# Splitting float32 weights into two interleaved halves, with activation tiles at shifted addresses, in a two-layer encoder

## The chip, the cores and the metric

The kernel runs on one core of one Trainium2 chip. The metric is the device time of one execution in microseconds (us); less is better.

## The reference, cut to what matters

A trunk of two layers on 512 tokens of width 1024, all in float32. Each layer is a pre-norm mixer with a residual add, and a last RMS norm closes the trunk. Layer 0 projects to a value and a gate half of width 2048 each, pools the values over trailing windows, mixes them by group, multiplies by the gate and projects back. Layer 1 (HGRN2) projects to four parts of width 2048 (query, forget gate, value, gate), runs a gated linear recurrence over 16 heads, and projects back.

```python
def pool_mixer(h, w_in, w_grp, scale, w_out):
    v, gate = split(h @ w_in)
    p = multiscale_pool(v)
    m = einsum('btgc,gcd->btgd', p, w_grp).reshape(B, T, D_INNER) * scale
    return (m * silu(gate)) @ w_out

def hgrn2_mixer(h, w_in, lb, norm_g, w_out):
    q, fz, i, gate = split(h @ w_in)
    o = scan(q, k(fz), i, log_f(fz))      # S_t = f_t S_(t-1) + k_t v_t, o_t = S_t q_t
    return (norm(o) * silu(gate)) @ w_out
```

## The kernel before

All products with weights are done as three matmuls. A float32 operand is split in a high half (the value rounded to the type float32r, which TensorE takes in one pass) and a low half (what is left): `split` (L93) lets ScalarE (ACT) cast the source to `hi` and VectorE (DVE) subtract `hi` from the source into `lo`. `mm3` (L125) then adds high by high (L126), high by low (L127) and low by high (L128) into one PSUM tile:

```python
def mm3(out, lh, ll, rh, rl, start, stop):
    nc.tensor.matmul(out, lh, rh, start=start, stop=False)
    nc.tensor.matmul(out, lh, rl, start=False, stop=False)
    nc.tensor.matmul(out, ll, rh, start=False, stop=stop)
```

The first operand of a matmul is the stationary one: 128 columns of it are loaded into the array by a weight load of its own (PEld in the profile). The second is the moving one, 512 columns here. In the profile's names, `mm<-xh,whi` is the moving `xh` and the stationary `whi`.

Weights come in pieces of 128 partitions by 1024 float32 columns (`piece`, L97; the first four pieces are loaded half by half at L219 to L230). Each piece has a raw tile `wraw` (4,096 bytes of each partition, 3 buffers) and two halves `whi` and `wlo` (4,096 bytes each, 6 buffers each), all of the pool `wpool`. SP's queue issues the load at L103 as soon as a raw buffer is free, ahead of its place in the program (`high_priority`).

The activations of a layer are scaled by the norm's gain and split in eight pairs `xh0`, `xl0` .. `xh7`, `xl7` of 512 columns (2,048 bytes) by `scaled_halves` (L197), once for each layer, in the pool `act`. `project` (L144) makes an output tile of 128 features by 512 tokens by running over the eight (or four) contraction tiles k with the weights stationary and the activations moving. `project4` does it for four output tiles at once, with k outermost. Three places have the roles turned, with activations stationary and weights moving: `inputs` (L394, the values of layer 1) and `out_half` (L345), which `add_out` and `finish` call. Between the products, DVE, ACT and GpSimd (POOL) work on the rows that come out (pooling, sigmoids, the recurrence's factors); TensorE also does the small 128-column products of the recurrence and the transposes.

SBUF is laid out pool after pool, tile after tile: 1,024 bytes of scratch for DMA descriptors, then `const`, `wpool`, `act`, `small`, and then the pool of the layer (`l0`, or the one of layer 1 in its place). Adding up the tiles' sizes gives their place in each partition. Taken modulo 256 bytes, the start of `whi` and `wlo` is 128, that of all `xh` and `xl` is 128, that of the pooled tiles `ph`, `pl` and the gated tiles `zh`, `zl` of layer 0 is 0, that of `z1h`, `z1l` of layer 1 is 128, and the pair `zz` of the last group is at 192 (high) and 0 (low). Slices within a tile start at multiples of 512 bytes.

Of the kernel before, what the change touches and what calls it, by code (L numbers as in the profile page):

```python
# [32 lines left out]
F32 = mybir.dt.float32  # L33
F32R = mybir.dt.float32r
# [6 lines left out]
P = 128  # L41
# [3 lines left out]
KD = D // P  # L45
KI = DI // P
NG = 4
GC = DI // NG
# [2 lines left out]
EPS = 1e-6  # L51
WINDOWS = (2, 4, 8, 16)
RAW, WB = 3, 6
WARM = 10
NORM_AT, SPREAD_AT = (KD - 2, 2), (KD - 1, 1)
AHEAD = 300
# [9 lines left out]
def trunk(ctx: ExitStack, tc: tile.TileContext, xT, par, ident_d, causal_d, mask_d, fg_d, w0_in, w0_grp, w0_out, w1_in, w1_out, out):  # L66
    nc = tc.nc
    const = ctx.enter_context(tc.tile_pool(name="const", bufs=1))
    wpool = ctx.enter_context(tc.tile_pool(name="wpool", bufs=1))
    act = ctx.enter_context(tc.tile_pool(name="act", bufs=1))  # L70
# [9 lines left out]
    warm = pa.tile([P, 512], F32, name="a", tag="a", bufs=4)  # L80
    for _ in range(WARM):
        nc.tensor.matmul(warm[:, :P], ones, ones, start=True, stop=True)
# [3 lines left out]
    nc.scalar.dma_start(out=pp, in_=par)  # L86
    ident = const.tile([P, P], F32, name="ident")
    mhalf = const.tile([P, 8], F32, name="mhalf")
    nc.gpsimd.memset(mhalf, -0.5)

    h = [const.tile([P, T], F32, name=f"h{k}") for k in range(KD)]

    def split(src, hi, lo):  # L93
        nc.scalar.copy(out=hi, in_=src)  # L94
        nc.vector.tensor_tensor(out=lo, in0=src, in1=hi, op=ALU.subtract)  # L95

    def piece(src):  # L97

        raw = wpool.tile([P, 2, GC], F32, name="wraw", tag="wraw", bufs=RAW)
        hi = wpool.tile([P, 2, GC], F32R, name="whi", tag="whi", bufs=WB)  # L100
        lo = wpool.tile([P, 2, GC], F32R, name="wlo", tag="wlo", bufs=WB)
        with tc.high_priority(AHEAD):
            nc.sync.dma_start(out=raw, in_=src)  # L103
            split(raw, hi, lo)
        return hi, lo

    def load_in(w, col=0):

        v = w.rearrange("(k p) n -> p k n", p=P)
        out = []  # L110
        for i in range(v.shape[1] // 2):
            hi, lo = piece(v[:, 2 * i:2 * i + 2, col:col + GC])
            out += [(hi[:, 0], lo[:, 0]), (hi[:, 1], lo[:, 1])]
        return out
# [15 lines left out]
    def project4(pieces, xs, norm):  # L130


        accs = [ps.tile([P, T], F32, name="mm", tag="mm", bufs=4) for _ in range(GT)]
        for k, ((wh, wl), (xh, xl)) in enumerate(zip(pieces, xs)):
            for n, acc in enumerate(accs):
                if (k, n) == NORM_AT:
                    rn = norm()
                if (k, n) == SPREAD_AT:
                    rb = spread_sbuf(rn)
                c = slice(n * P, (n + 1) * P)  # L140
                mm3(acc, wh[:, c], wl[:, c], xh, xl, k == 0, k == len(pieces) - 1)
        return accs, rn, rb

    def project(pieces, n, xs):  # L144

        acc = ps.tile([P, T], F32, name="mm", tag="mm", bufs=4)
        c = slice(n * P, (n + 1) * P)
        for k, ((wh, wl), (xh, xl)) in enumerate(zip(pieces, xs)):
            mm3(acc, wh[:, c], wl[:, c], xh, xl, k == 0, k == len(pieces) - 1)
        return acc  # L150
# [40 lines left out]
    def spread_sbuf(rn):  # L191
# [2 lines left out]
        nc.scalar.copy(out=rb, in_=spread(rn))  # L194
        return rb

    def scaled_halves(k, col):  # L197
        g = pp[:, col + k:col + k + 1]
        hi = act.tile([P, T], F32R, name=f"xh{k}", tag=f"xh{k}", bufs=1)
        lo = act.tile([P, T], F32R, name=f"xl{k}", tag=f"xl{k}", bufs=1)  # L200
        nc.scalar.activation(out=hi, in_=h[k], func=AF.Copy, scale=g)
        nc.vector.scalar_tensor_tensor(out=lo, in0=h[k], scalar=g, in1=hi, op0=ALU.mult, op1=ALU.subtract)
        return hi, lo

    def halves(src, tag, bufs, pool=act):
        hi = pool.tile([P, T], F32R, name=tag + "h", tag=tag + "h", bufs=bufs)
        lo = pool.tile([P, T], F32R, name=tag + "l", tag=tag + "l", bufs=bufs)
        split(src, hi, lo)
        return hi, lo
# [7 lines left out]
    with tc.tile_pool(name="l0", bufs=1) as l0:  # L217
        xs, pieces = [], []
        wv = w0_in.rearrange("(k p) n -> p k n", p=P)  # L219
        for i in range(4):  # L220
            raw = wpool.tile([P, 2, GC], F32, name="wraw", tag="wraw", bufs=RAW)
            hi = wpool.tile([P, 2, GC], F32R, name="whi", tag="whi", bufs=WB)
            lo = wpool.tile([P, 2, GC], F32R, name="wlo", tag="wlo", bufs=WB)
            for j in range(2):
                k = 2 * i + j
                nc.sync.dma_start(out=h[k], in_=xT[k * P:(k + 1) * P, :])
                nc.sync.dma_start(out=raw[:, j], in_=wv[:, k, 0:GC])
                xs.append(scaled_halves(k, C_NG0))
                split(raw[:, j], hi[:, j], lo[:, j])
                pieces.append((hi[:, j], lo[:, j]))  # L230
        nc.scalar.dma_start(out=ident, in_=ident_d)
        accs, _, rb = project4(pieces, xs, lambda: rms("l0", h))
        cnts = [C_CNT + sum(WINDOWS[:g]) for g in range(NG)]

        def values(g):
            vs = []
            wv = None if g == 0 else load_in(w0_in, g * GC)
            for n in range(GT):
                acc = accs[n] if g == 0 else project(wv, n, xs)
                v = l0.tile([P, 16 + T], F32, name="v", tag="v", bufs=4)  # L240
                nc.gpsimd.memset(v[:, 0:16], 0.0)
                nc.vector.tensor_tensor(out=v[:, 16:], in0=acc, in1=rb, op=ALU.mult)
                vs.append(v)
            return vs

        def pool(g, vs):
            w, out = WINDOWS[g], []
            for n in range(GT):
                cur, step = vs[n], 1
                while step < w:  # L250
                    nxt = l0.tile([P, 16 + T], F32, name="win", tag="win", bufs=2)
                    if 2 * step < w:
                        nc.gpsimd.memset(nxt[:, 0:16], 0.0)
                    nc.vector.tensor_tensor(out=nxt[:, 16:], in0=cur[:, 16:], in1=cur[:, 16 - step:16 + T - step], op=ALU.add)
                    cur, step = nxt, 2 * step
                nc.vector.tensor_tensor(out=cur[:, 16:16 + w], in0=cur[:, 16:16 + w], in1=pp[:, cnts[g]:cnts[g] + w], op=ALU.mult)
                p = small.tile([P, T], F32, name="p", tag="hg", bufs=2)
                nc.vector.scalar_tensor_tensor(out=p, in0=cur[:, 16:], scalar=1.0 / w, in1=vs[n][:, 16:], op0=ALU.mult, op1=ALU.subtract)
                out.append(halves(p, "p", 4, l0))
            return out  # L260

        def gates0(g):
            wg = load_in(w0_in, DI + g * GC)
            out = []
            for n in range(GT):
                acc = project(wg, n, xs)
                gt = l0.tile([P, T], F32, name="gt", tag="gt", bufs=2)
                nc.vector.tensor_tensor(out=gt, in0=acc, in1=rb, op=ALU.mult)
                sg = l0.tile([P, T], F32, name="sg", tag="sg", bufs=2)
                nc.scalar.activation(out=sg, in_=gt, func=AF.Sigmoid)  # L270
                gs = l0.tile([P, T], F32, name="gs", tag="gs", bufs=4)
                nc.gpsimd.tensor_tensor(out=gs, in0=gt, in1=sg, op=ALU.mult)  # L272
                out.append(gs)
            return out

        def mixed(g, ps_, gates):
            wm = load_in(w0_grp[g])
            out = []
            for n in range(GT):
                acc = project(wm, n, ps_)  # L280
                z = small.tile([P, T], F32, name="z", tag="hg", bufs=2)
                c = C_PS + g * GT + n
                nc.vector.scalar_tensor_tensor(out=z, in0=acc, scalar=pp[:, c:c + 1], in1=gates[n], op0=ALU.mult, op1=ALU.mult)
                out.append(halves(z, "z", 8, l0))
            return out

        zprev = None
        for g in range(NG):
            vs = values(g)
            px = pool(g, vs)  # L290
            if zprev is not None and g < NG - 1:
                project_out(load_out(w0_out, g - 1), zprev)
            gts = gates0(g)
            z = mixed(g, px, gts)
            if g == NG - 1:
                project_out(load_out(w0_out, g - 1), zprev)
            zprev = z
        project_out(load_out(w0_out, NG - 1), zprev)
# [482 lines left out]
```

## Time and profile before

| | us |
|---|---|
| median of 2 runs (842.31 to 843.68) | 842.99 |
| the profiled execution, its own time | 843.0 |
| its span in the profile | 841.2 |

Times in the rows below count from the start of the span. A matmul's duration in them overlaps the next one's; what tells how fast a row of matmuls runs is the distance between starts. The granted clock is a share of full speed: 1.00 is 2.4 GHz.

### The profile page before, as it was taken

To read this page: it belongs to the slowest core of one execution; us is meant where nothing else is said; L and a number is where in the kernel's file an instruction comes from. 1 tells how busy PE (TensorE), PEld (TensorE's weight loads), DVE (VectorE), ACT (ScalarE), POOL (GpSimd) and SP (SyncE) were. 2 spreads that over 40 slices of the span, in tenths; PEclk is the share of its full clock that TensorE was granted. 3 is DMA by queue.
4 is the path that set the end of the run, shared out by engine and by line. 5 is a ranking of instruction groups with operands and counts; after the bars stand their busy time and mean duration, and the time that the engine had idled before them with its cause. 6 is when DMAs were issued, how large, how long until landed. Compare 5 with 4: busy or idle time off the path is not lost.

```text
span 841.2 us, 10459 instructions
## 1 busy us (share of the span) xinstructions
PE 826.4 (98%) x4038; PEld 684.8 (81%) x4038; DVE 550.9 (65%) x837; ACT 275.2 (33%) x474; POOL 160.6 (19%) x204
## 2 busy tenths in 40 slices
PE   9899999999999999999999999999999999999995
PEld 7688888888888888888888888888888888888884
DVE  7766645753686456699269974459974459973744
ACT  7342224213323145323433240433240433242311
POOL 4020001001002013071223300213300213302100
PEclk9999999999999999999999999999999999999998
DMA  6622323122422245223032240332240333230202
GB/s 218 213 75 77 100 101 101 53 98 101 150 82 97 75 151 175 76 76 125 1 101 79 71 141 10 101 101 87 80 135 1 101 101 92 82 128 1 101 13 91
DMA packets 37194, 79.06 MB, mean 94 GB/s; under 512 B 2832, under 2 KB 3088, under 8 KB 37136
## 3 DMA queue, kind: packets, MB, share of 16 engines
q1 hardware_dynamic: 34688, 74.46, 27.1%
q10 hardware_dynamic: 2448, 3.86, 1.3%
q8 instruction: 33, 0.54, 0.3%
q14 instruction: 25, 0.20, 0.1%
HBM read 74.11 MB, written 4.19 MB: 93 GB/s over the span
## 4 chain that ended last, share of the span: by engine, by line
PE 95%; DVE 1%; DMA 1%; ACT 1%; issue 0%; POOL 0%; SPq 0%; POOLq 0%; DVEq 0%; ACTq 0%
PE mm L126 29%; PE mm L127 29%; PE mm L128 29%; PE a L556 2%; PE a L594 2%; PE a L574 1%; PE a L596 1%; PE a L563 1%; DMA wraw<-in_w0i 1%; PE a L438 1%; DVE wlo L95 1%; DMA h<-in_xT 0%; PE a L342 0%; ACT whi L94 0%; PE a L188 0%
## 5 line engine op out<-in xcount | busy, mean ns | idle before, releaser
L126 PE MATMUL mm<-xh,whi 128*128 128x512 f32 x640 | 251.2, 393 | 1.3 <-ACT whi L94 0.7
L128 PE MATMUL mm<-xh,wlo 128*128 128x512 f32 x640 | 249.7, 391 | 1.0 <-DVE wlo L95 1.0
L127 PE MATMUL mm<-xl,whi 128*128 128x512 f32 x640 | 249.7, 390 | 0.0
L94 ACT CAST whi<-wraw 128x1024 fp32r<-128x1024 f32 (+1 forms) x140 | 141.9, 1025 | 252.3 <-PE mm L127 115.5
L95 DVE TENSOR_TENSOR wlo<-wraw,whi 128x1024 fp32r<-128x1024 f32 (+1 forms) x140 | 172.7, 1261 | 57.6 <-ACT whi L94 56.6
L126 PEld LDWEIGHTS mm<-xh,whi 128*128 128x128 f32 x640 | 120.6, 188 | 27.1 <-ACT whi L94 1.4
L128 PEld LDWEIGHTS mm<-xh,wlo 128*128 128x128 f32 x640 | 120.4, 188 | 27.2 <-DVE wlo L95 2.0
L127 PEld LDWEIGHTS mm<-xl,whi 128*128 128x128 f32 x640 | 120.5, 188 | 24.5
L541 DVE RECIPROCAL r<-r 128x512 f32<-128x512 f32 x16 | 53.4, 3340 | 1.5 <-POOL r L540 1.5
L128 PE MATMUL mm<-zh,wlo 128*128 128x512 f32 x128 | 50.6, 395 | 0.0
L126 PE MATMUL mm<-zh,whi 128*128 128x512 f32 x128 | 50.6, 395 | 0.0
L127 PE MATMUL mm<-zl,whi 128*128 128x512 f32 x128 | 50.5, 395 | 0.0
L126 PE MATMUL mm<-whi,xh 128*128 128x512 f32 x128 | 50.1, 391 | 0.0
L128 PE MATMUL mm<-whi,xl 128*128 128x512 f32 x128 | 49.9, 390 | 0.0
L127 PE MATMUL mm<-wlo,xh 128*128 128x512 f32 x128 | 49.9, 390 | 0.0
L351 DVE TENSOR_TENSOR ht<-mm,ht 128x512 f32<-128x512 f32 x32 | 22.1, 689 | 35.5 <-PE mm L128 35.5
L214 DVE TENSOR_TENSOR h<-mm,h 128x512 f32<-128x512 f32 x32 | 22.0, 689 | 32.4 <-PE mm L128 32.3
L414 POOL TENSOR_TENSOR gs<-fz,s 128x512 f32<-128x512 f32 x16 | 21.4, 1336 | 98.6 <-ACT s L412 98.6
L272 POOL TENSOR_TENSOR gs<-gt,sg 128x512 f32<-128x512 f32 x16 | 21.3, 1330 | 92.4 <-ACT sg L270 92.3
L126 PE MATMUL mm<-whi,z1h 128*128 128x512 f32 x96 | 37.6, 392 | 0.0
L128 PE MATMUL mm<-whi,z1l 128*128 128x512 f32 x96 | 37.4, 389 | 0.0
L127 PE MATMUL mm<-wlo,z1h 128*128 128x512 f32 x96 | 37.4, 389 | 0.0
(141 smaller groups left out, 1164.9 us busy)
## 6 DMA issues: line engine op xcount, KB each, us to landing
wraw<-in_w1i SPq DMA_DIRECT2D x64, 512.0 KB, 3.9
wraw<-in_w0i SPq DMA_DIRECT2D x28, 512.0 KB, 4.2
wraw<-in_w0o SPq DMA_DIRECT2D x16, 512.0 KB, 3.9
wraw<-in_w1o SPq DMA_DIRECT2D x16, 512.0 KB, 4.3
wraw<-in_w0g SPq DMA_DIRECT2D x8, 512.0 KB, 4.1
h<-in_xT SPq DMA_DIRECT2D x8, 256.0 KB, 5.0
wraw<-in_w0i SPq DMA_DIRECT2D x8, 256.0 KB, 5.2
hmid<-h ACTq DMA_DIRECT2D x8, 256.0 KB, 2.3
```

The costliest lines, as they stand in the source:

```text
L94: nc.scalar.copy(out=hi, in_=src)
L95: nc.vector.tensor_tensor(out=lo, in0=src, in1=hi, op=ALU.subtract)
L126: nc.tensor.matmul(out, lh, rh, start=start, stop=False)
L127: nc.tensor.matmul(out, lh, rl, start=False, stop=False)
L128: nc.tensor.matmul(out, ll, rh, start=False, stop=stop)
L214: nc.vector.tensor_tensor(out=h[n], in0=acc, in1=h[n], op=ALU.add)
L272: nc.gpsimd.tensor_tensor(out=gs, in0=gt, in1=sg, op=ALU.mult)
L351: nc.vector.tensor_tensor(out=ht[b][:, c], in0=acc, in1=ht[b][:, c], op=ALU.add)
L414: nc.gpsimd.tensor_tensor(out=gs, in0=gt, in1=sg, op=ALU.mult)
L541: nc.vector.reciprocal(out=r, in_=r)
L556: nc.tensor.matmul(a[0:64, b], k[:, c:m], q[:, c:c + P], start=True, stop=True)
L594: nc.tensor.matmul(o[:, b], Ads[pr][:, j, t], v[:, b, n * P:(n + 1) * P], start=True, stop=b == 0)
```

## The change

The high and low half of a weight piece stand in one tile of 8,192 bytes, element by element: high half at every even float32, low half at every odd one. `hi` and `lo` are views of it with a step of 8 bytes, in all that reads or writes them. The order and number of instructions stay as they are. In `scaled_halves`, an unused tile of 32 bytes is allocated after each pair but the last, so that pair k starts 32·k bytes further than it would; both layers use the same tiles. A pad of 128 bytes in `const` and a DMA scratch that is 512 bytes smaller shift everything behind them.

```diff
--- before.py
+++ after.py
@@ -51,6 +51,7 @@
 EPS = 1e-6
 WINDOWS = (2, 4, 8, 16)
 RAW, WB = 3, 6
+PAD = 32
 WARM = 10
 NORM_AT, SPREAD_AT = (KD - 2, 2), (KD - 1, 1)
 AHEAD = 300
@@ -86,6 +87,7 @@
     nc.scalar.dma_start(out=pp, in_=par)
     ident = const.tile([P, P], F32, name="ident")
     mhalf = const.tile([P, 8], F32, name="mhalf")
+    const.tile([P, PAD], F32, name="pad")
     nc.gpsimd.memset(mhalf, -0.5)
 
     h = [const.tile([P, T], F32, name=f"h{k}") for k in range(KD)]
@@ -97,8 +99,8 @@
     def piece(src):
 
         raw = wpool.tile([P, 2, GC], F32, name="wraw", tag="wraw", bufs=RAW)
-        hi = wpool.tile([P, 2, GC], F32R, name="whi", tag="whi", bufs=WB)
-        lo = wpool.tile([P, 2, GC], F32R, name="wlo", tag="wlo", bufs=WB)
+        both = wpool.tile([P, 2, GC, 2], F32R, name="wb", tag="wb", bufs=WB)
+        hi, lo = both[..., 0], both[..., 1]
         with tc.high_priority(AHEAD):
             nc.sync.dma_start(out=raw, in_=src)
             split(raw, hi, lo)
@@ -194,10 +196,15 @@
         nc.scalar.copy(out=rb, in_=spread(rn))
         return rb
 
+    staggered = set()
+
     def scaled_halves(k, col):
         g = pp[:, col + k:col + k + 1]
         hi = act.tile([P, T], F32R, name=f"xh{k}", tag=f"xh{k}", bufs=1)
         lo = act.tile([P, T], F32R, name=f"xl{k}", tag=f"xl{k}", bufs=1)
+        if k < KD - 1 and k not in staggered:
+            staggered.add(k)
+            act.tile([P, 8], F32, name=f"step{k}")
         nc.scalar.activation(out=hi, in_=h[k], func=AF.Copy, scale=g)
         nc.vector.scalar_tensor_tensor(out=lo, in0=h[k], scalar=g, in1=hi, op0=ALU.mult, op1=ALU.subtract)
         return hi, lo
@@ -219,8 +226,8 @@
         wv = w0_in.rearrange("(k p) n -> p k n", p=P)
         for i in range(4):
             raw = wpool.tile([P, 2, GC], F32, name="wraw", tag="wraw", bufs=RAW)
-            hi = wpool.tile([P, 2, GC], F32R, name="whi", tag="whi", bufs=WB)
-            lo = wpool.tile([P, 2, GC], F32R, name="wlo", tag="wlo", bufs=WB)
+            both = wpool.tile([P, 2, GC, 2], F32R, name="wb", tag="wb", bufs=WB)
+            hi, lo = both[..., 0], both[..., 1]
             for j in range(2):
                 k = 2 * i + j
                 nc.sync.dma_start(out=h[k], in_=xT[k * P:(k + 1) * P, :])
@@ -771,7 +778,7 @@
         "in_w1i": f(hgrn_w_in)[0],
         "in_w1o": f(hgrn_w_out)[0],
     }
-    nc = bacc.Bacc("TRN2", target_bir_lowering=False, num_devices=1, dynamic_dma_scratch_size=1024)
+    nc = bacc.Bacc("TRN2", target_bir_lowering=False, num_devices=1, dynamic_dma_scratch_size=512)
     args = [nc.dram_tensor(n, a.shape, mybir.dt.from_np(a.dtype), kind="ExternalInput").ap() for n, a in arrays.items()]
     args.append(nc.dram_tensor("out_y", (T, D), F32, kind="ExternalOutput").ap())
     with tile.TileContext(nc) as tc:
```

## Rows read from the trace of the kernel before

**Rows 1.** Page, part 1: busy time of each engine
```profile
PE 826.4 (98%) x4038; PEld 684.8 (81%) x4038; DVE 550.9 (65%) x837; ACT 275.2 (33%) x474; POOL 160.6 (19%) x204
```

**Rows 2.** Page, part 4: chain that ended last, by engine and line
```profile
PE 95%; DVE 1%; DMA 1%; ACT 1%; issue 0%; POOL 0%; SPq 0%; POOLq 0%; DVEq 0%; ACTq 0%
```

**Rows 3.** Groups by line and shape: line, engine, out<-moving,stationary, xcount, busy, mean ns
```profile
L126 PE MATMUL mm<-xh,whi 128*128 128x512 f32 x640 | 251.2, 393 | 1.3 <-ACT whi L94 0.7 <-DVE v L242 0.5
...
L126 PE MATMUL mm<-zh,whi 128*128 128x512 f32 x128 | 50.6, 395 | 0.0
...
L126 PE MATMUL mm<-whi,xh 128*128 128x512 f32 x128 | 50.1, 391 | 0.0
...
L126 PE MATMUL mm<-whi,z1h 128*128 128x512 f32 x96 | 37.6, 392 | 0.0
...
L126 PE MATMUL mm<-ph,whi 128*128 128x512 f32 x64 | 25.3, 395 | 0.0
...
L126 PE MATMUL mm<-whi,zz 128*128 128x512 f32 x32 | 12.9, 402 | 0.0
```

**Rows 4.** Timeline of PE, 544.77 to 551.80: start us, us taken; 32 matmuls in a row
```profile
544.77 0.39 PE L127 MATMUL mm<-xl,whi 128*128 128x512 f32 x1
...
551.80 0.39 PE L128 MATMUL mm<-xh,wlo 128*128 128x512 f32 x1
```

**Rows 5.** Timeline of PE, 100.69 to 111.89; 49 matmuls in a row
```profile
100.69 0.40 PE L126 MATMUL mm<-zh,whi 128*128 128x512 f32 x1
...
111.89 0.40 PE L126 MATMUL mm<-zh,whi 128*128 128x512 f32 x1
```

**Rows 6.** Timeline of PE, 376.94 to 386.92; 45 matmuls in a row
```profile
376.94 0.39 PE L128 MATMUL mm<-whi,xl 128*128 128x512 f32 x1
...
386.92 0.39 PE L127 MATMUL mm<-wlo,xh 128*128 128x512 f32 x1
```

**Rows 7.** Timeline of PE, 820.11 to 824.96; 22 matmuls in a row
```profile
820.11 0.39 PE L127 MATMUL mm<-wlo,zz 128*128 128x512 f32 x1
...
824.96 0.39 PE L127 MATMUL mm<-wlo,zz 128*128 128x512 f32 x1
```

**Rows 8.** Groups by line and shape: two weight loads
```profile
L126 PEld LDWEIGHTS mm<-xh,whi 128*128 128x128 f32 x640 | 120.6, 188 | 27.1 <-ACT whi L94 1.4 <-DVE v L242 1.0 <-DVE h L214 0.2
...
L557 PEld LDWEIGHTS a<-q,kk 128*64 128x64 f32 x128 | 10.4, 135 | 0.0
```

**Rows 9.** Windows: us, busy us of each engine (instructions), granted clock, DMA share, GB/s
```profile
545.00:552.00 7.00, 7.00 (x32) 5.82 (x31) 1.38 (x2) 0.97 (x2) 1.30 (x1) 1.00 0.00 0
101.00:112.00 11.00, 11.00 (x49) 8.86 (x48) 2.77 (x4) 0.79 (x1) 0.00 (x0) 1.00 0.01 1
0.00:20.00 20.00, 17.94 (x80) 14.85 (x81) 15.15 (x23) 15.79 (x27) 9.10 (x17) 1.00 0.65 229
```

**Rows 10.** Groups by line and shape: the two instructions that split a weight piece
```profile
L95 DVE TENSOR_TENSOR wlo<-wraw,whi 128x1024 fp32r<-128x1024 f32 x132 | 165.6, 1282 | 57.1 <-ACT whi L94 56.0
L94 ACT CAST whi<-wraw 128x1024 fp32r<-128x1024 f32 x132 | 137.1, 1050 | 252.3 <-PE mm L127 115.5 <-PE mm L128 61.6 <-DMA wraw<-in_w1i 33.4
```

**Rows 11.** Timeline of DVE, first and last product of one sweep, widths 1 and 32
```profile
358.16 0.42 DVE L526 TENSOR_TENSOR f<-f 128x256 f32<-128x256 f32 x1
...
361.51 0.42 DVE L526 TENSOR_TENSOR f<-f 128x256 f32<-128x256 f32 x1
```

**Rows 12.** Page, part 3: the two queues that carry data
```profile
q1 hardware_dynamic: 34688, 74.46, 27.1%
q10 hardware_dynamic: 2448, 3.86, 1.3%
```

**Rows 13.** Waits of the SP queue: for whom, us in total, times, longest
```profile
SPq L103 <- DVE wlo L95: 627.6, 122, 33.1
```

**Rows 14.** Page, part 2: DVE's busy tenths in 40 slices of the span
```profile
DVE  7766645753686456699269974459974459973744
```

## The prediction

> **What bounds the kernel now.** First the page's busy times: TensorE's matmuls fill 826.4 of 841.2 us, DVE 550.9, ACT 275.2 [rows 1]. The chain that ended last is PE for 95% [rows 2], so a microsecond counts where TensorE's stream gets shorter. The reader should then look for idle time before the matmuls: beside the 640 matmuls of one kind stand 1.3 us, beside the others 0.0 [rows 3]. TensorE does not wait for operands; it runs its matmuls one after another at their own pace, and that pace is what to study.
>
> The pace is in the timeline. With `x` moving, 31 distances between starts take 551.80 − 544.77 = 7.03 us, 226.8 ns each [rows 4]. With `z` moving, 48 distances take 11.20 us, 233.3 ns [rows 5]. With the weights moving and `x` stationary, 44 distances take 9.98 us, 226.8 ns [rows 6]; with `zz` stationary 21 take 4.85 us, 231.0 ns [rows 7]. The granted clock is 1.00, 2.4 GHz, in the first two stretches, and hardly any other engine works there: DVE 1.38 of 7.00 us, DMA share 0.00 [rows 9]. So neither the clock nor other traffic makes 226.8 into 233.3. The instructions are alike; what differs is the place of the operands. `x` (128 modulo 256 bytes) runs beside loads of weights that start at 128, difference 0; `z` (at 0) runs beside weights at 128, difference 128; `zz` has differences 64 and 128. `z1`, whose distance from the weights is also a multiple of 256, takes the mean time of `x` in the same role, 392 and 391 ns, and `zz` 402 [rows 3]. The pace thus depends on the operands' addresses modulo 256 bytes.
>
> If one column enters per clock, 512 columns take 512 / 2.4 = 213.3 ns; that floor is an estimate. `x` then has an excess of 13.5 ns, `z` and `p` 20.0. A weight load runs beside the matmul ahead of it. Loads of 128 and 64 columns take 188 and 135 ns [rows 8]: 53 / 64 = 0.83 ns per column, 106 ns for 128. A load thus walks through 4 / 0.83 = 4.8 bytes per ns, the moving operand through 4 bytes in 0.417 ns, 9.6 bytes per ns. In 106 ns the stream makes four rounds of 256 bytes and the load two, so the stream overtakes the load twice. Read this way, an overtaking costs 13.5 / 2 = 6.7 ns for `x` and 10 for `z`.
>
> The row shows a dependence on addresses, 226.8 against 233.3 [rows 4, 5]. The Trainium skill, "TensorE: Matmul & The Clock Gate", "Step-by-step: what each phase is for", says the contrary: the two operands have read ports of their own, and loading the next tile's weights takes no bandwidth from the running matmul. By the rows the layout can be worth up to 20 ns a matmul; by that rule it is worth nothing, and the time stays at 843.
>
> **The change part by part.** *Stationary weights.* 640 + 128 + 64 = 832 groups of three matmuls, as L127 and L128 repeat L126's counts [rows 3]: 1,920 with `x` moving, 576 with `z` or `p`. The load now steps 8 bytes per column: 8 / 0.83 = 9.6 bytes per ns, the speed of the moving stream. Neither overtakes the other. Their distance modulo 256 stays what it was at the start: −32·k for `x` of pair k, and for `z` and `p` 160, since the weights' start comes to 0 (128 − 512 + 128) and theirs to 96 (0 − 512 + 128 + 224). One `x` pair in eight starts on the same place as the load; it should meet once and then follow behind. Lower end: all excess goes, 213.3 ns. Upper end: a load now spans 1,024 bytes instead of 512, and if the excess goes by bytes spanned it doubles, to 240.3 and 253.3. I take a quarter of `x`'s excess as left, 213.3 + 3.4 = 216.7 ns for all, because the rows speak for meetings as the price and at least one shift of eight still meets. Gain: 1,920 · 10.1 = 19.4 us, and 576 · 16.6 = 9.6 us; 29.0 together.
>
> *Moving weights.* 128 + 96 + 32 = 256 groups, 768 matmuls [rows 3]. The stream now walks at 19.2 bytes per ns beside a load at 4.8: eight rounds against two, six meetings instead of two, each a third as long (14.4 against 4.8 bytes per ns of difference). Lower end: no excess, 213.3. Upper end: an operand with a step of 8 bytes is delivered at half speed, 426.6 ns; no row has such an operand. I take the nearest row, a weights-moving stretch with an unfavourable place, 231.0 [rows 7], against 226.8 [rows 6]: 768 · 4.2 = 3.2 us lost.
>
> A page that bears on the upper end: the Trainium skill, "SBUF — State Buffer", "Door 1: The DMA port swizzle", gives lines of 16 bytes and asks two hits on each for full bandwidth. A float32 operand with a step of 8 bytes has just two, so by it the half speed does not come; no run here shows that for TensorE.
>
> *The split.* 132 ACT casts (1,050 ns) and 132 DVE subtractions (1,282 ns) [rows 10] now write, and DVE also reads, with a step of 8 bytes. DVE's product of width 1 has that step in its output and one input and takes 0.42 us, as does that of width 32, which has runs of 32 [rows 11]. So I take 0 for both. Upper end: DVE doubles, +165.6 us on an engine with 550.9. What covers that is SP's queue, which waits 627.6 us for raw buffers, so loads run as far ahead as buffers allow [rows 13]. In DVE's fullest slices, four of nine tenths [rows 14], there is no such cover: doubled, four slices of 21 us would add some 20 to 40 us. The lower end is 0, for nothing is removed.
>
> *What is late next.* In those four of 40 slices DVE may hold back what TensorE gains: 4/40 of 25.8 is 2.6 us, which I subtract from the gain. The first 20 us, with DVE at 15.15 and ACT at 15.79 [rows 9], are the split's own and stay. *Scratch, pad and steps* move addresses only: all of the kernel's data goes over the two queues named hardware_dynamic [rows 12] before and after; I price the smaller scratch at 0, with SP's 627.6 us of waiting as cover should a load start late [rows 13].
>
> *Sum.* 843.0 (own time of the profiled execution, equal to the median 842.99 within 0.1) − 29.0 + 3.2 + 2.6 = 819.8, say 820 us.
>
> **Rivals.** (a) *The layout does nothing for TensorE*: the 13.5 ns are a fixed price per matmul and only the difference between 0 and 128 is about addresses. For it: no row shows a stretch below 226.8 [rows 4, 6], so that pace may hold no meeting at all. Against it: 233.3 and 231.0 show that meetings have a price [rows 5, 7]. The time: 843, or 576 · 6.5 = 3.7 us less if `z` and `p` fall to `x`'s pace: 839 to 843. The page on TensorE quoted above gives the same result.
>
> (b) *Half speed of the interleaved operand when it moves.* Place: `inputs`, `add_out`, `finish`. Price: 768 · (426.6 − 226.8) = 153.4 us; with the gain of 29.0 the time is 843.0 + 153.4 − 29.0 = 967. It decides from 29.0 / 768 = 38 ns on: a pace above 264.6 there and the change loses. For it: no row shows a step of 8 bytes in a matmul, and TensorE takes 512 columns in 227 ns [rows 4] where DVE takes 256 elements in 420 [rows 11], so what DVE can bear may be too much for it. Against it: DVE's products of width 1, which lose nothing by the step [rows 11].
>
> (c) *More lines, more conflicts.* A load that spans twice the bytes doubles its price: 1,920 · 13.5 + 576 · 20.0 = 37.4 us, and 768 · 13.5 = 10.4 us for the moving side, 891 us. For it: excess exists on each of the four paces. Against it: 226.8 and 231.0 differ with the place at equal spans, so span alone is not the price.
>
> (d) *DVE or ACT slows with the step*: 820 + 20 to 40 us, 840 to 860.
>
> **How the numbers follow.** Forecast 0.52, (a) 0.17, (b) 0.13, (c) 0.13, (d) 0.05. The forecast's own range is 800 to 832: the lower end has all stationary excess gone (1,920 · 13.5 + 576 · 20.0 = 37.4) and part of the moving side's 10.4, the upper end half of the gain. The range 797 to 892 leaves out (b) and little else. A measurement of this kernel can tell about 2%, 17 us, from no change. Faster by over 2% (under 826): 0.51, nearly all of the forecast's case. Within 2%: 0.20, from (a) and weak forms of the forecast. Slower: 0.29, from (b), (c) and part of (d).
>
> **What would show it.** Right: distances between starts of about 217 ns for `x`, `z` and `p` alike, and near 231 or less with weights moving; the casts at 1,050 and the subtractions at 1,282 ns as before; the same counts. Wrong: 226.8 again (a), over 264 in `inputs` and `add_out` (b), 240 and more with stationary weights (c), longer splits with new idle time before L126 and L128 (d). If `x` shows a pace that differs from pair to pair, the shift matters and the streams keep their distance; if all eight pairs agree, the equal speeds alone do it.

## The result, and the profile after

The changed kernel takes 1027.06 us (1025.96 to 1028.16, 2 runs) against 842.99 before: a ratio of 1.218, interval 1.216 to 1.220. It is slower by 184 us, far outside the range, and on the other side of the forecast. The profiled execution has a span of 1024.2 us, 183.0 more than before.

Where those 183 us went can be read in four steps. First the page's busy times, then its chain by engine:

```profile
PE 1009.9 (99%) x4038; PEld 718.9 (70%) x4038; DVE 557.4 (54%) x837; ACT 287.0 (28%) x474; POOL 164.2 (16%) x204
```

```profile
PE 96%; DVE 1%; DMA 1%; ACT 1%; issue 0%; POOL 0%; POOLq 0%; DVEq 0%; ACTq 0%
```

Against [rows 1], PE grew from 826.4 to 1009.9 us, by 183.5, while DVE grew by 6.5 and ACT by 11.8. The chain is PE's for 96%, as it was for 95% [rows 2]. So the same 4,038 matmuls got slower; nothing new is waited for. The groups by line and shape say which (L126 of before is L128 here, and both halves have the name `wb`; L95 and L94 are L97 and L96):

```profile
L128 PE MATMUL mm<-xh,wb 128*128 128x512 f32 x640 | 255.1, 399 | 0.5 <-ACT wb L96 0.5
...
L97 DVE TENSOR_TENSOR wb<-wraw,wb 128x1024 fp32r<-128x1024 f32 x132 | 166.6, 1276 | 155.4 <-ACT wb L96 153.7
L96 ACT CAST wb<-wraw 128x1024 fp32r<-128x1024 f32 x132 | 149.0, 1136 | 339.7 <-PE mm L130 262.8 <-DMA wraw<-in_w1i 31.4 <-DMA wraw<-in_w0i 21.8
...
L128 PE MATMUL mm<-wb,xh 128*128 128x512 f32 x128 | 82.6, 645 | 0.0
...
L128 PE MATMUL mm<-wb,z1h 128*128 128x512 f32 x96 | 62.4, 650 | 0.0
...
L128 PE MATMUL mm<-wb,zz 128*128 128x512 f32 x32 | 20.4, 637 | 0.0
```

Those with `x` moving went from 393 to 399 ns, those with the weights moving from 391, 392 and 402 to 645, 650 and 637 [rows 3]. DVE's subtraction did not change (1,276 against 1,282 ns), ACT's cast takes 1,136 instead of 1,050 [rows 10]. Durations overlap, so the price is read from the distance between starts, in the timeline of PE. A stretch with `x` moving, 189 distances in 43.94 us:

```profile
225.86 0.39 PE L128 MATMUL mm<-xh,wb 128*128 128x512 f32 x1
...
269.80 0.40 PE L128 MATMUL mm<-xh,wb 128*128 128x512 f32 x1
```

That is 232.5 ns, where [rows 4] gave 226.8. A stretch with `z` moving, 90 distances in 21.00 us:

```profile
91.93 0.40 PE L129 MATMUL mm<-zl,wb 128*128 128x512 f32 x1
...
112.93 0.40 PE L129 MATMUL mm<-zl,wb 128*128 128x512 f32 x1
```

233.3 ns, as in [rows 5]. A stretch with the weights moving and `x` stationary, 59 distances in 26.72 us:

```profile
513.08 0.65 PE L128 MATMUL mm<-wb,xh 128*128 128x512 f32 x1
...
539.80 0.65 PE L130 MATMUL mm<-wb,xl 128*128 128x512 f32 x1
```

452.9 ns, where [rows 6] gave 226.8. In the last group, with `zz`, 55 distances take 24.93 us, 453.3 ns, where [rows 7] gave 231.0. Two windows, one within the first of these stretches and one over the third, show (us, busy us of each engine, granted clock, DMA share, GB/s) that the clock stayed at its upper level, 1.00, and that hardly anything else was busy in the slow one:

```profile
235.00:260.00 25.00, 25.00 (x109) 20.98 (x108) 22.01 (x33) 7.72 (x9) 2.55 (x10) 1.00 0.26 85
513.00:540.00 27.00, 27.00 (x61) 12.46 (x60) 4.51 (x7) 4.13 (x6) 1.23 (x1) 1.00 0.07 20
```

The sum goes by the mean distance between neighbours of one kind over the whole of each trace, without those that a pause makes over a fifth longer than the middle value. With the weights moving it is 227.6 ns before and 453.4 after, with `x` moving 226.9 and 232.5, with `z` and `p` 233.3 and 233.4. So 768 · 225.8 = 173.4 us come from moving weights, 1,920 · 5.6 = 10.8 us from `x`, nothing from `z` and `p`: 184.2 us for the 183.0 that the span grew.

### The profile page after: what moved, and what is told of

Read it like the earlier page. It is cut to its first block, busy times and chain, and to the rows that moved or that the text cites. A ratio compares the mean times of both kernels' runs of the same rounds, so it can differ in the third digit from the quotient of the medians.

```text
span 1024.2 us, 10458 instructions
## 1 busy us (share of the span) xinstructions
PE 1009.9 (99%) x4038; PEld 718.9 (70%) x4038; DVE 557.4 (54%) x837; ACT 287.0 (28%) x474; POOL 164.2 (16%) x204
## 4 chain that ended last, share of the span: by engine, by line
PE 96%; DVE 1%; DMA 1%; ACT 1%; issue 0%; POOL 0%; POOLq 0%; DVEq 0%; ACTq 0%
PE mm L128 30%; PE mm L129 30%; PE mm L130 30%; PE a L601 1%; PE a L563 1%; PE a L603 1%; PE a L581 1%; PE a L570 1%; DMA wraw<-in_w0i 1%; PE a L445 1%; DVE wb L97 0%; PE a L349 0%; DVE xl L209 0%; DMA pp<-in_par 0%; ACT wb L96 0%
## 5 line engine op out<-in xcount | busy, mean ns | idle before, releaser
L97 DVE TENSOR_TENSOR wb<-wraw,wb 128x1024 fp32r<-128x1024 f32 (+1 forms) x140 | 173.8, 1255 | 156.0 <-ACT wb L96 154.3
L128 PE MATMUL mm<-xh,wb 128*128 128x512 f32 x640 | 255.1, 399 | 0.5 <-ACT wb L96 0.5
L130 PE MATMUL mm<-xh,wb 128*128 128x512 f32 x640 | 252.8, 395 | 1.3 <-DVE wb L97 1.3
L129 PE MATMUL mm<-xl,wb 128*128 128x512 f32 x640 | 253.4, 396 | 0.0
L96 ACT CAST wb<-wraw 128x1024 fp32r<-128x1024 f32 (+1 forms) x140 | 154.1, 1108 | 339.7 <-PE mm L130 262.8
L130 PEld LDWEIGHTS mm<-xh,wb 128*128 128x128 f32 x640 | 125.4, 196 | 26.0 <-DVE wb L97 2.0
L128 PEld LDWEIGHTS mm<-xh,wb 128*128 128x128 f32 x640 | 124.8, 195 | 24.9 <-ACT wb L96 0.7
L129 PEld LDWEIGHTS mm<-xl,wb 128*128 128x128 f32 x640 | 125.3, 196 | 23.4
L128 PE MATMUL mm<-wb,xh 128*128 128x512 f32 x128 | 82.6, 645 | 0.0
L129 PE MATMUL mm<-wb,xh 128*128 128x512 f32 x128 | 82.5, 644 | 0.0
L130 PE MATMUL mm<-wb,xl 128*128 128x512 f32 x128 | 82.4, 644 | 0.0
L128 PE MATMUL mm<-wb,z1h 128*128 128x512 f32 x96 | 62.4, 650 | 0.0
L129 PE MATMUL mm<-wb,z1h 128*128 128x512 f32 x96 | 62.2, 648 | 0.0
L128 PE MATMUL mm<-zh,wb 128*128 128x512 f32 x128 | 50.7, 396 | 0.0
L130 PE MATMUL mm<-zh,wb 128*128 128x512 f32 x128 | 50.4, 394 | 0.0
L128 PEld LDWEIGHTS mm<-wb,xh 128*128 128x128 f32 x128 | 26.5, 207 | 30.4 <-issue 30.4
```

## The experiments

**1. The weights that move, half after half.** Undoes one part: the pieces of `inputs`, `add_out` and `finish` hold their halves apart, in the same tiles; the rest is the changed kernel.

```diff
+        if moves:
+            both = wpool.tile([P, 2, 2, GC], F32R, name="wb", tag="wb", bufs=WB)
+            hi, lo = both[:, 0], both[:, 1]
+        else:
+            both = wpool.tile([P, 2, GC, 2], F32R, name="wb", tag="wb", bufs=WB)
+            hi, lo = both[..., 0], both[..., 1]
```

> The changed kernel, but the weight pieces that move (those of inputs, add_out and finish) stand half after half in their tile; the others stay interleaved, and the shifts stay. Theory 1, the step of 8 bytes halves the pace of a moving operand: 768 matmuls go back from 453 to some 227 ns, 173 us less, so 850 to 857 us, and what is left over 843 is the 233 instead of 227 ns of the matmuls with x moving. Theory 2, the loads and the stream collide more since twice the bytes are spanned: moving the halves apart changes only one of the two operands, and the time stays above 900 us. Theory 3, the split on ACT and DVE got slower: nearly no change, 1000 us or more.

Measured: 857.58 us (856.11 to 858.45), 1.017 of before (1.016 to 1.019). That is half a microsecond over the upper end of theory 1, which stands: 169.5 us of the 184 come back with that part alone. Theories 2 and 3 fall, for the loads are still interleaved, and so is the split of all other pieces (ACT's cast still takes 1,120 ns on the mean). The timeline of PE in the same place of the program (weights moving, `z1` stationary), 94 distances in 22.01 us:

```profile
512.75 0.48 PE L132 MATMUL mm<-wb,z1h 128*128 128x512 f32 x1
...
534.76 0.40 PE L133 MATMUL mm<-wb,z1h 128*128 128x512 f32 x1
```

234.1 ns, with one short pause in it, instead of some 453. What is left, 14.5 us over the kernel before, is neither the step of the moving operand nor the split: the mean distances, 232.5 ns with `x` moving and 232.2 with weights moving, are 1,920 · 5.6 = 10.8 and 768 · 4.6 = 3.5 us above those of before.

**2. The shifts alone.** The kernel before with the steps, the pad and the smaller scratch, and nothing interleaved.

```diff
+    const.tile([P, PAD], F32, name="pad")
...
+        if k < KD - 1 and k not in staggered:
+            staggered.add(k)
+            act.tile([P, 8], F32, name=f"step{k}")
```

> The kernel before with the shifts, the pad and the smaller scratch alone; halves in tiles of their own. If the place modulo 256 bytes sets the pace whatever the step of the weights, x leaves its good place for seven pairs of eight: about 230 ns on the mean instead of 226.7, 1920 times, so 847 to 853 us, and each pair has a pace of its own. If the shifts matter only beside an interleaved load, 841 to 845 us.

Measured: 858.54 us (856.67 to 859.37), 1.017 of before (1.016 to 1.019): as much as experiment 1, and 5.5 us over the upper end of what was expected. So the shifts have a price without any interleaving. PE's timeline where `x` moves, 189 distances in 43.96 us:

```profile
228.87 0.39 PE L128 MATMUL mm<-xh,whi 128*128 128x512 f32 x1
...
272.83 0.40 PE L128 MATMUL mm<-xh,whi 128*128 128x512 f32 x1
```

232.6 ns, against 226.8 where `x` and the weights start at the same place. The row takes the pairs in order, three matmuls each, so the distances can be sorted by pair: the means go from 231.0 ns (pair 1) to 234.3 (pair 5). Pair 0 has 231.5, although by the layout its difference from the weights is 0 as before. So in a row whose places change, the pace of a matmul does not follow from its own difference alone. That rows of one difference have different paces is shown by experiments 4 and 5; how the pairs of a mixed row act on each other is not.

**3. The interleaving alone.** The changed kernel without steps, pad and smaller scratch, so that all high halves of the weights and all `x` start at the same place again (the low halves, interleaved, start 4 bytes further).

```diff
-    const.tile([P, PAD], F32, name="pad")
...
-            act.tile([P, 8], F32, name=f"step{k}")
```

> The changed kernel without shifts, pad and smaller scratch. Theory 1, the step of the moving operand: 768 matmuls stay at about 453 ns, so 1010 to 1030 us. Whether x comes back to 226.7 ns (about 1015 us) or stays near 233 (about 1027 us) tells whether the shifts or the step of the load cost its 6 ns. If equal speeds of load and stream had been good for anything, a place where both start alike would show it here at its worst.

Measured: 1025.99 us (1025.93 to 1028.46), 1.218 of before (1.216 to 1.220), the time of the changed kernel. PE's timeline where `x` moves, 189 distances in 44.09 us:

```profile
225.84 0.39 PE L126 MATMUL mm<-xh,wb 128*128 128x512 f32 x1
...
269.93 0.39 PE L126 MATMUL mm<-xh,wb 128*128 128x512 f32 x1
```

233.3 ns. So `x` does not come back: an interleaved load at the good place costs as much as a plain load at a middling one. The two 6 ns do not add up. Interleaving takes the good place away, and the shifts then find nothing more to spoil. The cast also shows that its price belongs to the interleaving and not to the shifts:

```profile
L94 ACT CAST wb<-wraw 128x1024 fp32r<-128x1024 f32 x132 | 148.9, 1135 | 340.0 <-PE mm L128 259.8 <-DMA wraw<-in_w1i 32.3 <-DMA wraw<-in_w0i 21.2
```

**4. The paces by themselves.** Rows of 24 matmuls on constant tiles, one kind after another; no layer is computed. The stationary operand is loaded anew for each. There is one execution of this program, and one of that of experiment 7.

```python
for name, st, mv in tests:
    ...
    for i in range(REPS):
        nc.tensor.matmul(o, st, mv, start=i == 0, stop=i == REPS - 1)
```

> Only rows of 24 matmuls of 128 by 512 float32r on constant tiles, one kind after another; none of the layers is computed. Contiguous operands at equal places: 226.7 ns. Theory 1, the stream's own pace has one part in sixteen on top of 512 columns at 2.4 GHz, loads only add to it at bad places: a load that reads one address only (same) stays at 226.7, a moving step of 8 bytes takes 453 with and without such a load, 256 columns take 113.3, 384 take 170. Theory 2, the 13 ns over 213.3 come from meetings with the load: same falls to 213 to 216, a moving step of 8 bytes to 427 beside it, 384 columns keep 13 ns over 160. If what is fetched at once is 8 bytes, runs of two elements with gaps of two are back at 227; if it is a line of 16 bytes, runs of four are and runs of two stay at 453.

Mean of the last 18 distances between starts of each kind, ns, by the profile's records:

```
contiguous, 0 32 64 96 128 160 192 224 bytes off:  226.7 233.4 228.9 233.7 233.3 234.4 233.3 233.3
load that reads one address only:                  231.1
load with a step of 8 bytes, 0 32 64 128 192 off:  233.3 233.3 233.3 231.6 229.8
load with a step of 16 bytes:                      234.9
moving step of 8 bytes; beside the one-address load:  453.4  451.1
moving step of 16 bytes:                           461.2
moving in runs of 2, 4, 8, 64 elements, equal gaps: 453.2 233.3 233.6 226.7
384 and 256 moving columns:                        173.8  119.7
bfloat16 operands:                                 215.8
```

Kinds stand one after another in the timeline, so most of these paces are also the distance between two of its rows over 24 matmuls:

```profile
65.66 5.72 PE L119 MATMUL same<-mov,sta 128*128 128x512 f32 x24
71.21 28.05 PE L119 MATMUL sta2at<-mov,sta 128*128 128x512 f32 x120
99.10 5.80 PE L119 MATMUL sta<-mov,sta 128*128 128x512 f32 x24
104.74 11.08 PE L119 MATMUL mov<-mov,sta 128*128 128x512 f32 x24
115.63 11.01 PE L119 MATMUL mov2same<-mov,sta 128*128 128x512 f32 x24
126.46 11.25 PE L119 MATMUL mov<-mov,sta 128*128 128x512 f32 x24
137.53 27.77 PE L119 MATMUL runs<-mov,sta 128*128 128x512 f32 x96
```

The load of one address runs from 65.66 to 71.21, 231.3 ns. The moving step of 8 bytes runs from 104.74 to 115.63, 453.8 ns, and beside the one-address load to 126.46, 451.3. Steps of 16 bytes take 235.0 in the load (99.10 to 104.74) and 461.3 when they move (126.46 to 137.53). With no layer, no DMA and no other engine, the step of 8 bytes takes twice 226.7. Theory 1 is right on that. On the rest both theories failed in part. A load of one address is no cheaper (231.1), where theory 1 expected 226.7 and theory 2 213 to 216. And 384 columns take 13.8 ns over 160, 256 take 13.0 over 106.7: about a fixed amount, as theory 2 had it, and not the sixteenth part that theory 1 named.

What keeps the stream from half pace is a run of four elements, 16 bytes (233.3): runs of two with gaps of two are as slow as single elements. Runs of three, and runs of four that begin elsewhere than at a multiple of 16 bytes, were not tried. The bytes spanned do not do it, as runs of 2, 4, 8 and 64 all span as much as the step of 8. Nor does the number of 16-byte blocks touched, as a step of 16 bytes touches twice the blocks of a step of 8 and takes only 461.

**5. Layer 0's activations at the weights' place.** One unused tile, the other way round: `ph`, `pl`, `zh` and `zl` move from difference 128 to 0.

```diff
     with tc.tile_pool(name="l0", bufs=1) as l0:
+        l0.tile([P, 32], F32, name="pad0")
         xs, pieces = [], []
```

> The kernel before with one unused tile of 128 bytes at the head of layer 0's pool, so that ph, pl, zh and zl start at 128 modulo 256 as the weights do. If equal places set the good pace: the 576 matmuls that move them go from 233.3 to about 226.8 ns, 3.8 us less, 838 to 841 us. If those tiles run at 233 for another reason: 842 to 844 us.

Measured: 839.68 us (839.50 to 840.28), 0.9957 of before (0.9943 to 0.9971). PE's timeline where `z` moves, 89 distances in 20.18 us:

```profile
91.70 0.39 PE L127 MATMUL mm<-zl,whi 128*128 128x512 f32 x1
...
111.88 0.39 PE L126 MATMUL mm<-zh,whi 128*128 128x512 f32 x1
```

226.7 ns instead of 233.3 [rows 5], as expected; 576 · 6.6 = 3.8 us. This version beats both kernels, the one before by 0.43% (its slowest run, 840.28, is below the fastest of before, 842.79), with 128 bytes and no other edit.

**6. Interleaved by 16 bytes.** The kernel before with the moving weights interleaved in runs of four elements. Everything else stands apart, at the places of before.

```diff
+            both = wpool.tile([P, 2 * GC // RUN, 2, RUN], F32R, name="wb", tag="wb", bufs=WB)
+            hi, lo = both[:, :, 0], both[:, :, 1]
```

> The kernel before with only the weight pieces that move interleaved, and in runs of four elements (16 bytes of the high half, 16 of the low one) instead of element by element; no shifts. If single elements 8 bytes apart are what halves the stream: 768 matmuls at about 233 instead of 227 ns, so 846 to 850 us. If the doubled span of the moving operand or the interleaving in itself does it: 453 ns and about 1016 us.

Measured: 846.99 us (846.89 to 847.64), 1.0043 of before (1.0027 to 1.0058). PE's timeline where the weights move, 74 distances in 17.19 us:

```profile
479.62 0.40 PE L143 MATMUL mm<-wb,xh 128*128 128x512 f32 x1
...
496.81 0.39 PE L142 MATMUL mm<-wb,xh 128*128 128x512 f32 x1
```

232.3 ns. The span of the moving operand is the same as in the changed kernel, the halves are interleaved, and yet 3.8 us came where 768 matmuls at 453 ns cost 173.4. What halves the stream in the changed kernel is that its elements stand singly, 8 bytes apart.

**7. What the load costs.** Loads of different widths beside the same stream, and more places.

```python
tests += [(f"wide{w}", sta[:, 0:w], mov[:, 0:512]) for w in (128, 96, 64, 32)]
tests += [(f"slow{w}", sta[:, 0:w], step2) for w in (128, 64, 32)]
tests += [("third", s1, step3)]
tests += [(f"by{4 * k:04d}", s1, mov[:, k:k + 512]) for k in (0, 1, 2, 4, 64, 128, 512)]
```

> Rows of 24 matmuls on constant tiles again, none of the layers is computed: loads of 128, 96, 64 and 32 columns beside 512 contiguous moving columns, the same beside a moving step of 8 bytes, a moving step of 12 bytes, and a contiguous moving operand that starts 0, 4, 8, 16, 256, 512 and 2048 bytes off. If the 13.3 ns over 213.3 are paid per 16 bytes loaded, one column's time each: 226.7, 223.3, 220.0, 216.7 ns, and 453, 440, 433 beside the slow stream. If they are a fixed price of a matmul: 226.7 for all widths. A step of 12 bytes takes about 453 to 461 ns if every step above 4 bytes runs at one element in 0.83 ns, about 340 to 640 if the pace follows the bytes. Starts 256, 512 and 2048 bytes off are as good as 0 if the period is 256 bytes.

Means as in experiment 4, ns:

```
load of 128, 96, 64, 32 columns, contiguous stream:  226.7 229.8 230.0 231.6
the same beside a moving step of 8 bytes, 128 64 32: 451.1 451.1 452.8
moving step of 12 bytes:                             465.3
contiguous, 0 4 8 16 256 512 2048 bytes off:         226.7 236.7 233.3 232.0 226.7 226.7 226.7
bfloat16 operands:                                   215.8
```

```profile
15.26 22.21 PE L105 MATMUL wide<-mov,sta 128*128 128x512 f32 x96
37.30 32.69 PE L105 MATMUL slow<-mov,sta 128*128 128x512 f32 x72
69.80 11.38 PE L105 MATMUL third<-mov,sta 128*128 128x512 f32 x24
80.97 38.84 PE L105 MATMUL by<-mov,sta 128*128 128x512 f32 x168
```

The four widths together run from 15.26 to 37.30: 22.04 us over 96 matmuls, 229.6 ns. A load of a quarter of the columns is no cheaper for the stream than the full one, even dearer. So the 13 ns are not paid per column or byte loaded, and the price per 16 bytes falls; nor is the pace the same for all widths. The step of 12 bytes, from 69.80 to 80.97, takes 465.4 ns, a little over the 453 to 461 expected: steps of 8, 12 and 16 bytes cost about the same. Starts 256, 512 and 2,048 bytes off are as good as 0, and an offset of 4 bytes is the worst of those tried (236.7).

## Why the prediction was wrong

**What bounds the kernel** was read rightly. The pace of TensorE's stream sets the time, the clock and the other engines do not, and the pace depends on addresses modulo 256 bytes. Experiment 5 shows the last by itself.

**The step that failed first** is "I take the nearest row, a weights-moving stretch with an unfavourable place, 231.0". That row has a contiguous operand, so it bounds the price of a place and not of a step. The term of 3.2 us measured 173.4. The upper end named for it, half speed and 426.6 ns, was the case; it came out at 453.4, so the excess over the computed floor doubled too, from 13 to 27 ns. The mechanism was on record as rival (b), with 967 us, but with a chance of 0.13 it stayed outside the range. No row of before had a matmul operand with a step, and DVE's products of width 1 [rows 11], which spoke for no loss, take 420 ns for 256 elements. They say nothing of an engine that takes 512 in 227.

A page spoke against the half speed: the Trainium skill, "SBUF — State Buffer", "Door 1: The DMA port swizzle", asks two hits on each 16-byte line for full bandwidth. The runs differ from it where a matmul's moving operand is float32r: two elements of each line, by steps or by runs of two, take 453 ns, and one element of each line takes 461. Four take 233. The measurement decides.

**The step that failed second** is the reading of the 13.5 ns as two overtakings at 6.7 ns, and from it the gain of 29.0 us. The stationary side lost 10.8: `x` went to 232.5 ns and `z` and `p` stayed at 233.4, all forecast at 216.7. Two runs speak against that reading. A load of 32 columns, which would be over in a quarter of the time, leaves 231.6 (experiment 7), and an interleaved load, which by the reading keeps pace with the stream, gives 229.8 to 233.3 at all places tried (experiment 4). The load of one address (231.1) does not decide, as the stream would pass a fixed address too. In all runs 226.7 was the best settled pace of 512 contiguous float32r columns, and `x` had it already. The excess of `x` was a floor, by all layouts tried, taken for a loss; only the 6.6 ns of `z` and `p` were to be had, 3.8 us in all, and the change did not give them that, since it moved them to difference 160 beside interleaved loads, and no such load reached 226.7 at any place tried. Rival (a) said this of `x`, with a best case of 839. That is the time of experiment 5, but the change does not lead there.

**The rest.** The Trainium skill, "TensorE: Matmul & The Clock Gate", "Step-by-step: what each phase is for", has the load take nothing from the running matmul. The place costs 6.5 ns a matmul in [rows 5] against [rows 4], and up to 10 in experiment 7 without any other engine, so in this the trace does not agree. DVE's split stayed at 1,276 ns as forecast, ACT's cast grew by 86 ns where 0 was forecast; it is off the path, where ACT has 1% of the chain as before. That DVE's full slices would hold back a gain could not show, as there was none; the row has eight such slices, in four pairs, and not four [rows 14], so the 2.6 us for them should have been 5.2. The smaller scratch and the pad show no cost of their own: experiment 3, without them and the steps, takes the time of the changed kernel. In experiment 2, 1,920 · 5.6 ns = 10.8 us with `x` moving and 768 · 4.7 = 3.6 us with weights moving make 14.4 of the 15.4 us that were measured.

**What stays open** is what the 13 ns consist of. They are nearly the same for 256, 384 and 512 columns, a narrower load adds 3 to 5, they double when the stream runs at half pace, and bfloat16 operands pay 2.5. The trace of experiment 4 has one more hint: its first contiguous matmuls start 427 ns apart before the row settles at 227, and 512 columns at the lower clock level, 1.2 GHz, would take 426.7, with no excess. The clock's rows read 1.00 there, so that this was the lower level is not shown. Why an equal place modulo 256 bytes is the good one, and why a shorter load loses it, was not found either.

## What to carry to other kernels

Look at how each operand is used before changing its layout: a float32r operand that moves through TensorE kept its pace within 3% with runs of 16 bytes, and single elements 8, 12 or 16 bytes apart halve the pace, while a step of 8 or 16 bytes in a stationary operand cost 1% to 4%. Before an excess over a computed floor is counted as a gain, measure that floor with a row of matmuls on constant tiles; here it would have shown that the best pace was already reached. Where all moving and stationary tiles of a row start at the same place modulo 256 bytes, float32r matmuls of 512 columns ran 1% to 4% faster than at the other places tried, and a small unused tile can bring that about.

## What was not expected of the hardware

- In the cases tried the moving pace has two levels and no slope between them: 453 ns for a step of 8 bytes, 465 for 12, 461 for 16, 453 for runs of two; 233 for runs of four and eight; 227 for runs of 64 and for contiguous columns.
- An offset of 4 bytes between moving and stationary operand costs 10 ns (236.7 against 226.7), more than one of 32 to 224.
- A load of fewer columns, or of one address, makes the matmul beside it slower: 231.6 for 32 columns, 231.1 for one address, 226.7 for the full load.
- ACT's cast of 1,024 elements takes 86 ns more when it writes every other float32; DVE's subtraction, which reads and writes so, takes no more.
